# Seven half-sized products in the place of eight for every other pair of feature blocks

## The chip, the core and the metric

The kernel runs on one core of a Trainium2 chip, in one launch. The metric is the device time in microseconds. PE is TensorE (matmuls), DVE VectorE, ACT ScalarE, POOL GpSimd, SP the engine that issues the DMAs.

## What is computed

One sequence of 512 tokens with 1024 features goes through a first block (two kinds of attention, then an MLP) and through two layers of a second block, each a swiglu, a mixer of three branches and a second swiglu. All is float32. The parts that the change touches are the MLP (once) and the swiglu (four times):

```python
# first block
h2 = rmsnorm(x, ln2_g[l])
x = x + jnp.square(jax.nn.relu(h2 @ w_up[l])) @ w_down[l]      # 1024 -> 4096 -> 1024
...
def _swiglu(u, wi, wo):
    a, g = jnp.split(u @ wi, 2, axis=-1)                        # 1024 -> 2 x 1408
    return (jax.nn.silu(a) * g) @ wo                            # 1408 -> 1024
...
for l in range(DEPTH_2):
    x = x + 0.5 * _swiglu(_rms_norm(x, ffn1_norm[l]), ffn1_wi[l], ffn1_wo[l])
    ...   # the mixer
    x = x + 0.5 * _swiglu(_rms_norm(x, ffn2_norm[l]), ffn2_wi[l], ffn2_wo[l])
```

## The kernel before

x is kept in SBUF by feature: eight blocks of 128 features on the partitions, 512 tokens along them. A float32 product is made of three matmuls of type float32r: every operand is split into hi, its rounded value, and lo, the rest, and `mm3` (line 389) adds hi·hi, hi·lo and lo·hi into one PSUM bank. The split costs one ACT instruction (hi, a cast) and one DVE instruction (lo, a subtraction): for x in `split_x`, with the gain g of the norm, giving `xh` and `xl`; for weights in `load_w`, which fetches `wraw` in pieces of 128 x 1024 numbers and makes `whi` and `wlo`; for results in `split_to`. There are two raw buffers and four of whi and of wlo, taken in turn (WB).

`fm` makes one block of 128 output features for all 512 tokens: eight blocks of input features times three matmuls of 512 columns, 24 in all. The norm's factor for each token is not known when x is split; `norm_job` finds it while PE works on (a chain of small DVE instructions from the PSUM tile `ssq` to the tiles `dg`, from which the matmul `bcps` spreads it over the partitions as `Rrow`). Evacuations that need `Rrow` are held until then (`hold`), and released in one go.

`swiglu` (line 570) has eleven steps j. Each loads 128 columns of a and 128 of g, makes `pa` and `pg`, and evacuates: DVE multiplies both by `Rrow`, ACT takes silu, POOL multiplies the two, and the result is split into hidh and hidl. `mlp` (line 609) has three groups gi of 11, 11 and 10 blocks. Each group loads two blocks at a time, makes `pu` for each, and evacuates with relu and `Rrow` on DVE (`r`), a square on ACT (hidh), a square on POOL (`rq`) and a subtraction on DVE (hidl); then `down` multiplies the group's hid by w_down and adds to x.

Larger tiles live in `Slots`: 22 places of 4096 bytes a partition (kind D), given out by the first free place in a list and put back at its end. PE's instructions keep the order in which the code is written, where `Loom` weaves side jobs in at fixed points; the other engines' order is set by a list scheduler, and each engine serves its own instructions strictly in that order.

Of the kernel before, what the change touches and what calls it, by code (L numbers as in the profile page):

```python
# [19 lines left out]
KB = 8  # L20
# [3 lines left out]
FFN = 1408  # L24
# [4 lines left out]
def dram(t, off, ap):  # L29
    return bass.AP(tensor=t.tensor, offset=t.offset + off, ap=ap)  # L30
# [125 lines left out]
class Net:  # L156
    def __init__(self, ctx, tc, a):
        self.tc, self.nc, self.a = tc, tc.nc, a
        P = lambda name, bufs, **k: ctx.enter_context(tc.tile_pool(name=name, bufs=bufs, **k))
        self.const = P("const", 1)  # L160
        self.wp = P("wp", 2)
        self.act = P("act", 1)
        self.sc = P("sc", 2)
        self.tiny = P("tiny", 2)
        self.ps = P("ps", 8, space=PSUM)
        ctx.enter_context(tc.manual_schedule(engines={mybir.EngineType.PE}))
        self.loom = Loom()
# [8 lines left out]
        self.odd = False  # L176
        self.make_consts()


# [21 lines left out]
        return self.ps.tile([128, S], F32, name=name, tag="ps")  # L201


    def mm(self, out, lhsT, rhs, start, stop):
        self.nc.tensor.matmul(out, lhsT, rhs, start=start, stop=stop)  # L205
# [337 lines left out]
    def square(self, tb, t, ssq):  # L543
        A = self.nc.scalar
        junk = self.H.get("xj", [128, D])
        A.activation(junk, t, AF.Square, accum_out=ssq[:, tb:tb + 1])
        self.H.put(junk, t)

    def x_tok_job(self, out):
        for tb in range(TB):  # L550
            yield lambda: self.H.room(4096)
            t = self.H.get("xtok", [128, D])
            for h in range(2):
                ps = self.bank("xtp")
# [4 lines left out]
            yield 10.0  # L559

    def split_to(self, hi, lo, t):
        self.nc.scalar.copy(hi, t)
# [4 lines left out]
        hp = [self.pair("hid") for _ in range((n + 1) // 2)]  # L567
        return hp, self.blocks(hp, n)

    def swiglu(self, wi):  # L570
        nc = self.nc
        hp, hid = self.hid(11)
        for j in range(11):
            parts = self.load_w(wi, 2 * FFN, 0, KB, j * 128, 128, FFN + j * 128)
            pa, pg = self.bank("pa"), self.bank("pg")
            self.fm(parts, self.xs, 0, pa)
            self.fm(parts, self.xs, 1, pg)

            def evac(j=j, pa=pa, pg=pg):
                t1 = self.scr("t1")  # L580
                t2 = self.scr("t2")
                nc.vector.tensor_mul(t1, pa, self.rrow)
                nc.scalar.activation(t1, t1, AF.Silu)
                nc.vector.tensor_mul(t2, pg, self.rrow)
                nc.gpsimd.tensor_mul(t2, t2, t1)  # L585
                self.split_to(hid[j][0], hid[j][1], t2)
            self.hold(evac)
        return hp, hid
# [19 lines left out]

    def mlp(self, wu, wd, g_next):
        nc = self.nc  # L610
        j0 = 0
        for gi, n in enumerate((11, 11, 10)):
            hp, hid = self.hid(n)
            j = 0
            while j < n:
                w = min(2, n - j)
                parts = self.load_w(wu, 4096, 0, KB, (j0 + j) * 128, 128 * w)
                for i in range(w):
                    ps = self.bank("pu")
                    self.fm(parts, self.xs, i, ps)  # L620

                    def evac(ps=ps, hi=hid[j + i][0], lo=hid[j + i][1]):
                        r = self.scr("r")
                        q = self.scr("rq")
                        nc.vector.scalar_tensor_tensor(r, ps, 0.0, self.rrow, op0=ALU.max, op1=ALU.mult)
                        nc.gpsimd.tensor_mul(q, r, r)
                        nc.scalar.activation(hi, r, AF.Square)
                        nc.vector.tensor_sub(lo, q, hi.bitcast(F32))
                    self.hold(evac)
                j += w  # L630
            if gi == 2:
                self.g = g_next
            self.down(hid, wd, j0 * 128, 1.0, gi == 2)
            self.H.put(*sum(hp, ()))
            j0 += n
# [433 lines left out]
    def ffn2(self, l, which, g_next, last=False):  # L1069
        a = self.a  # L1070
        wi, wo = a[f"ffn{which}_wi_2"][l], a[f"ffn{which}_wo_2"][l]
        xtok = []
        if which == 1:
            b = a["b_in_2"][l]
            self.lcols = self.columns("lcols", [(dram(b, 0, []), 2), (dram(b, 256, []), 2), (dram(b, 768, []), 8),
                                                (dram(b, 3240, []), 24), (a["ml_conv_b_2"][l], 8), (a["ml_conv_w_2"][l], 32),
                                                (a["mla_q_norm_2"][l], 2), (a["mla_kv_norm_2"][l], 1)], 30.0)
        if last:
            self.loom.add(self.x_tok_job(xtok))
        hp, hid = self.swiglu(wi)  # L1080
# [580 lines left out]
    def everything(self):  # L1661
# [43 lines left out]
WB = (2, 4)  # L1705
```

## Time and profile before

| | us |
|---|---|
| median of 3 runs | 2325.81 (2325.63 to 2326.12) |
| the profiled execution | 2324.79 |
| its span, from the first to the last instruction | 2323.1 |
| PE busy | 2308.8 (99%), 10884 matmuls |
| DVE busy | 1293.6 (56%) |
| ACT busy | 907.3 (39%) |
| POOL busy | 381.3 (16%) |

A row of the timeline gives the start in us from the span's start, the duration, the engine, the line, the operation, the tiles as out<-in, and in brackets how long the engine sat idle before it and what it waited for. Matmuls overlap, so that their durations add up to more than the time they take. The MLP runs from 378.4 us to 723.9, the first swiglu starts there, the one behind the mixer of layer 0 at 1341.3.

### The profile page before, as it was taken

The numbers are of one execution on the slowest core, as the hardware profiler recorded it, in microseconds if no ns is written. First come the engines' busy times: TensorE is split into PE (matmuls) and PEld (weight loads), VectorE is DVE, ScalarE is ACT, GpSimd is POOL, SyncE is SP. The second block draws the span as 40 slices with busy tenths as digits, with TensorE's granted clock in tenths as the row PEclk, the third lists the DMA queues.
The fourth block names the chain that finished last, engine by engine and source line by source line (L and its number), as shares of the span: only waits on it lengthen the run. The fifth ranks groups of instructions, "written<-read, shape, count | busy, mean of one in ns | idle before, by whom it ended". The sixth has DMA issues, their size and how long they took to land.

```text
span 2323.1 us, 28438 instructions
## 1 busy us (share of the span) xinstructions
PE 2308.8 (99%) x10884; PEld 1913.4 (82%) x10884; DVE 1293.6 (56%) x2255; ACT 907.3 (39%) x1509; POOL 381.3 (16%) x385
## 2 busy tenths in 40 slices
PE   8999999999999999999999999999999999999999
PEld 7898888888888888877888888888888778888887
DVE  7844556444355545678564555455457674646552
ACT  6655432222223233656533333223236672333331
POOL 2000024101022112111111311211211101213110
PEclk9999999999999999999999999999999999999999
DMA  4223333233323323313323333333233142323332
GB/s 139 65 64 87 105 100 93 91 99 101 98 86 105 99 89 95 102 55 91 105 64 91 109 91 91 100 92 100 91 102 91 46 114 73 88 83 105 93 100 87
DMA packets 250524, 213.68 MB, mean 92 GB/s; under 512 B 14230, under 2 KB 234132, under 8 KB 250388
## 3 DMA queue, kind: packets, MB, share of 16 engines
q1 hardware_dynamic: 250388, 211.87, 30.6%
q8 instruction: 85, 1.39, 0.2%
q14 instruction: 51, 0.42, 0.1%
HBM read 208.64 MB, written 3.19 MB: 91 GB/s over the span
## 4 chain that ended last, share of the span: by engine, by line
PE 98%; DVE 1%; DMA 0%; ACT 0%; issue 0%; SPq 0%; ACTq 0%
PE pgate L205 15%; PE pd L205 15%; PE pt L205 14%; PE pg L205 10%; PE pa L205 10%; PE pu L205 8%; PE pf L205 6%; PE po L205 6%; PE pbr L205 5%; PE mls L205 1%; PE mnum L205 1%; PE sbl L205 1%; PE mss L205 1%; PE dio L205 1%; PE s L205 1%; PE pT L212 0%
## 5 line engine op out<-in xcount | busy, mean ns | idle before, releaser
L385 DVE TENSOR_TENSOR wlo<-wraw,whi 128x1024 fp32r<-128x1024 f32 (+3 forms) x394 | 550.8, 1398 | 414.1 <-ACT whi L384 409.8
L384 ACT CAST whi<-wraw 128x1024 fp32r<-128x1024 f32 (+3 forms) x394 | 404.3, 1026 | 657.2 <-PE pg L205 141.7
L205 PE MATMUL pd<-hidh,wlo 128*128 128x512 f32 x520 | 202.4, 389 | 0.0
L205 PE MATMUL pd<-hidl,whi 128*128 128x512 f32 x520 | 202.4, 389 | 0.0
L205 PE MATMUL pd<-hidh,whi 128*128 128x512 f32 x520 | 202.4, 389 | 0.0
L205 PE MATMUL pgate<-xh,whi 128*128 128x512 f32 x512 | 201.5, 394 | 0.0
L205 PE MATMUL pgate<-xh,wlo 128*128 128x512 f32 x512 | 199.6, 390 | 0.0
L205 PE MATMUL pgate<-xl,whi 128*128 128x512 f32 x512 | 199.4, 389 | 0.0
L205 PE MATMUL pt<-whi,xh 128*128 128x512 f32 (+2 forms) x480 | 182.2, 380 | 0.1
L205 PE MATMUL pt<-whi,xl 128*128 128x512 f32 (+2 forms) x480 | 172.5, 359 | 0.0
L205 PE MATMUL pt<-wlo,xh 128*128 128x512 f32 (+2 forms) x480 | 172.3, 359 | 0.0
L205 PE MATMUL pa<-xl,whi 128*128 128x512 f32 x352 | 137.3, 390 | 0.7 <-DVE xl L474 0.7
L205 PE MATMUL pa<-xh,whi 128*128 128x512 f32 x352 | 137.7, 391 | 0.0
L205 PE MATMUL pg<-xh,whi 128*128 128x512 f32 x352 | 137.5, 391 | 0.0
L205 PE MATMUL pa<-xh,wlo 128*128 128x512 f32 x352 | 137.2, 390 | 0.0
L205 PE MATMUL pg<-xh,wlo 128*128 128x512 f32 x352 | 137.1, 390 | 0.0
L205 PE MATMUL pg<-xl,whi 128*128 128x512 f32 x352 | 137.1, 389 | 0.0
L585 POOL TENSOR_TENSOR t<-t,t 128x512 f32<-128x512 f32 x44 | 56.8, 1290 | 426.5 <-ACT whi L384 303.8
L205 PEld LDWEIGHTS pd<-hidl,whi 128*128 128x128 f32 x520 | 97.6, 188 | 20.4
L205 PEld LDWEIGHTS pd<-hidh,whi 128*128 128x128 f32 x520 | 97.6, 188 | 20.2
L205 PEld LDWEIGHTS pd<-hidh,wlo 128*128 128x128 f32 x520 | 97.6, 188 | 20.1
L205 PEld LDWEIGHTS pt<-whi,xh 128*128 128x128 f32 x480 | 102.7, 214 | 13.0 <-issue 3.0
(519 smaller groups left out, 4612.8 us busy)
## 6 DMA issues: line engine op xcount, KB each, us to landing
wraw<-in_w_in_dram SPq DMA_DIRECT2D x116, 512.0 KB
wraw<-in_ffn_wi_dram SPq DMA_DIRECT2D x176, 256.0 KB
wraw<-in_ffn_wo_dram SPq DMA_DIRECT2D x34, 512.0 KB
wraw<-in_w_up_dram SPq DMA_DIRECT2D x32, 512.0 KB
wraw<-in_w_out_dram SPq DMA_DIRECT2D x24, 512.0 KB
wraw<-in_w_down_dram SPq DMA_DIRECT2D x24, 512.0 KB
wraw<-in_w_in_dram SPq DMA_DIRECT2D x32, 256.0 KB
wraw<-in_ffn_wo_dram SPq DMA_DIRECT2D x12, 384.0 KB
```

What stands on the lines that cost most here:

```text
L205: self.nc.tensor.matmul(out, lhsT, rhs, start=start, stop=stop)
L384: nc.scalar.copy(hi, raw)
L385: nc.vector.tensor_sub(lo, raw, hi.bitcast(F32))
L585: nc.gpsimd.tensor_mul(t2, t2, t1)
```

## The change

Two blocks of output features and the two halves of the tokens form a 2 x 2 product: x by halves of features and tokens (A11, A12, A22 and so on, 512 features by 256 tokens), the weights by halves of features and the two blocks (E11, E21, E22, ...). `seven` makes the four results by seven products of quarters instead of eight. It needs sums of quarters of x (S2, N1, S3, S4), which `forms` makes and splits once for each MLP and swiglu, and sums of quarters of the weights (T1 to T4 in the tiles tA and tB), which `load_sums` makes on DVE for each pair before they are split. Each product is 4 x 3 matmuls of 256 columns into half a bank. The order of the products on PE is A11·E11 (bank a), S2·T2 (b), A22·T4 (d), N1·T1 (c), A12·E21 (added onto a, once ACT has copied it as s1, a half of the tile m7), S3·T3 (added onto b, once DVE has made u2, the other half of m7), and later S4·E22 (added onto c, once DVE has read it). The seventh is put off into the next block (`later`, `flush`). A swiglu pair is the a and the g block of one step, for j = 2, 4, 6, 8; an MLP pair is two neighbouring blocks, for seven of the sixteen pairs. The sums of x hold eight places of kind D until the last pair; tA and tB hold two more from the loading of a pair to its splits.

```diff
@@ -386,11 +387,11 @@
-    def mm3(self, ps, whi, wlo, xhi, xlo, first, last):
-
-        self.mm(ps, whi, xhi, first, False)
-        self.mm(ps, whi, xlo, False, False)
-        self.mm(ps, wlo, xhi, False, last)
+    def mm3(self, ps, whi, wlo, xhi, xlo, first, last, **k):
+
+        self.mm(ps, whi, xhi, first, False, **k)
+        self.mm(ps, whi, xlo, False, False, **k)
+        self.mm(ps, wlo, xhi, False, last, **k)
...
+    def forms(self):
...
+        names = ("S2", "N1", "S3", "S4")
+        self.sums = {n: tuple(H.get("sum" + n, [128, 4, 256], F32R) for _ in range(2)) for n in names}
+        half = slice(0, 256), slice(256, 512)
+        for i in range(2):
+            f = {n: self.scr("f" + n).rearrange("p (k c) -> p k c", c=256) for n in names}
+            t = self.scr("ft").rearrange("p (k c) -> p k c", c=256)
+            for j in range(2):
+                k1, k2 = 2 * i + j, 4 + 2 * i + j
+                x = lambda k, h: self.x[:, k, half[h]]
+                A.activation(t[:, j], x(k1, 1), AF.Copy, scale=g[:, k1:k1 + 1])
+                for n, k, h, sc, other in (("N1", k2, 1, g, t), ("S2", k1, 0, ng, f["N1"]), ("S3", k1, 0, g, t),
+                                           ("S4", k2, 0, ng, f["S2"])):
+                    V.scalar_tensor_tensor(f[n][:, j], x(k, h), sc[:, k:k + 1], other[:, j], op0=ALU.mult, op1=ALU.subtract)
+            for n in names:
+                hi, lo = (y[:, 2 * i:2 * i + 2] for y in self.sums[n])
+                self.split_to(hi, lo, f[n])
...
+    def load_sums(self, w, ncol, c0, c1):
...
+        (r1, v1), (r2, v2) = E
+        ta, tb = (H.get(n, [128, 2, 4, 128]) for n in ("tA", "tB"))
+        V.tensor_add(ta[:, 1], v1[:, :, 1], v2[:, :, 1])
+        V.tensor_add(tb[:, 0], ta[:, 1], v1[:, :, 0])
+        V.tensor_add(tb[:, 1], tb[:, 0], v2[:, :, 0])
+        V.tensor_add(ta[:, 0], v1[:, :, 0], v1[:, :, 1])
...
+        A.copy(h11, v1[:, :, 0])
+        V.tensor_sub(l11, v1[:, :, 0], h11.bitcast(F32))
...
+        split(flat(tb), 1024, ("T2", "T4"), lambda i, k: i * 512 + k * 128)
+        split(flat(ta), 1024, ("T1", "T3"), lambda i, k: i * 512 + k * 128)
+        split(r2, 1024, ("E21", "E22"), lambda i, k: k * 256 + i * 128)
+        H.put(ta, tb)
+        return out
+
+    def seven(self, w, ncol, c0, c1, u, v, done):
...
+        W = self.load_sums(w, ncol, c0, c1)
+        a, b, c, d = (self.bank("ps7")[:, 0:256] for _ in range(4))
+        m = self.scr("m7")
+        s1, u2 = m[:, 0:256], m[:, 256:512]
+        u3 = self.scr("u7")[:, 0:256]
+
+        def prod(ps, q, e, first):
+            for k in range(4):
+                self.mm3(ps, *W[e][k], *self.quarters[q][k], first and k == 0, k == 3, skip_group_check=not first)
+            self.loom.turn()
+        prod(a, "A11", "E11", True)
+        A.copy(s1, a)
+        self.flush()
+        prod(b, "S2", "T2", True)
+        V.tensor_add(u2, b, s1)
+        prod(d, "A22", "T4", True)
+        prod(c, "N1", "T1", True)
+        prod(a, "A12", "E21", False)
+        prod(b, "S3", "T3", False)
+        V.tensor_add(u3, b, s1)
+        V.scalar_tensor_tensor(v[:, 256:512], c, -1.0, u3, op0=ALU.mult, op1=ALU.subtract)
+        V.tensor_add(u[:, 256:512], d, u3)
+
+        def rest():
+            prod(c, "S4", "E22", False)
+            V.scalar_tensor_tensor(v[:, 0:256], c, -1.0, u2, op0=ALU.mult, op1=ALU.subtract)
+            done(a)
+        self.later.append(rest)
...
+    def swiglu(self, wi, last):
...
         for j in range(11):
+            if j == 1:
+                self.forms()
+            if j in SEVEN:
+                self.loom.wait(lambda: self.normed)
...
+                self.seven(wi, 2 * FFN, j * 128, FFN + j * 128, t1, t2, done)
...
             self.fm(parts, self.xs, 0, pa)
+            self.flush()
...
             while j < n:
                 w = min(2, n - j)
+                if gi == 0 and j == 2:
+                    self.forms()
+                if w == 2 and (gi, j) in SEVEN_MLP:
+                    self.loom.wait(lambda: self.normed)
...
+                    self.seven(wu, 4096, c, c + 128, u, v, done)
...
                     self.fm(parts, self.xs, i, ps)
+                    self.flush()
...
+            self.flush()
             if gi == 2:
+                self.drop_forms()
...
+SEVEN = (2, 4, 6, 8)
+SEVEN_MLP = {(0, 4), (0, 8), (1, 0), (1, 4), (1, 8), (2, 2), (2, 6)}
```

In the last swiglu the job that transposes x back to tokens moves from the beginning to the steps behind the last pair.

Three places in the order of the instructions follow. The first is DVE in the MLP's first group, from the evacuations that were held for `Rrow`. Before (pu is a block's result, rq POOL's square):

```order
L467 COPY Rrow_3682<-bcps_3679 128x512
L625 SCALAR_TENSOR_TENSOR r_3684<-pu_3576,Rrow_3682 128x512
L625 SCALAR_TENSOR_TENSOR r_3690<-pu_3601,Rrow_3682 128x512
L628 TENSOR_TENSOR hidl_3553<-rq_3685,hidh_3552 128x512
L625 SCALAR_TENSOR_TENSOR r_3708<-pu_3666,Rrow_3682 128x512
L628 TENSOR_TENSOR hidl_3553<-rq_3691,hidh_3552 128x512
```

With the change, DVE from the split of the first pair's E21 and E22 (wlo_3826) to u2 (m7_3833, made of bank b, ps7_3830, and s1):

```order
L564 TENSOR_TENSOR wlo_3826<-wraw_3805,whi_3825 128x1024
L759 TENSOR_TENSOR hidl_3553<-rq_3742,hidh_3552 128x512
L787 SCALAR_TENSOR_TENSOR r_3746<-pu_3601,Rrow_3738 128x512
L386 TENSOR_TENSOR wlo_3914<-wraw_3912,whi_3913 128x1024
L759 TENSOR_TENSOR hidl_3553<-rq_3748,hidh_3552 128x512
L787 SCALAR_TENSOR_TENSOR r_3764<-pu_3722,Rrow_3738 128x512
L583 TENSOR_SCALAR ng_11597<-gains_327 128x8
L787 SCALAR_TENSOR_TENSOR r_3795<-pu_3770,Rrow_3738 128x512
L386 TENSOR_TENSOR wlo_3920<-wraw_3918,whi_3919 128x1024
L759 TENSOR_TENSOR hidl_3555<-rq_3766,hidh_3554 128x512
L759 TENSOR_TENSOR hidl_3555<-rq_3797,hidh_3554 128x512
L666 TENSOR_TENSOR m7_3833<-ps7_3830,m7_3833 128x256
```

All four held evacuations and the next two weight splits stand between the pair's last weights and u2.

The second place is ACT at the same point. Before, casts of weights and squarings of the held blocks:

```order
L384 CAST whi_3746<-wraw_3745 128x1024
L384 CAST whi_3752<-wraw_3751 128x1024
L627 ACTIVATE hidh_3552<-r_3684 128x512
L627 ACTIVATE hidh_3552<-r_3690 128x512
L627 ACTIVATE hidh_3554<-r_3708 128x512
L384 CAST whi_3820<-wraw_3819 128x1024
```

With the change, ACT from the cast of E21 and E22 to s1 (m7_3833, the copy of bank a, ps7_3829):

```order
L563 CAST whi_3825<-wraw_3805 128x1024
L385 CAST whi_3913<-wraw_3912 128x1024
L758 ACTIVATE hidh_3552<-r_3740 128x512
L758 ACTIVATE hidh_3552<-r_3746 128x512
L385 CAST whi_3919<-wraw_3918 128x1024
L758 ACTIVATE hidh_3554<-r_3764 128x512
L758 ACTIVATE hidh_3554<-r_3795 128x512
L663 COPY m7_3833<-ps7_3829 128x256
```

The copy s1 stands behind the four squarings and behind the casts of the next two pieces of weights.

The third place is DVE where the MLP's second group follows on down of the first; pd_4286 and pd_4321 (pd_4464 and pd_4499 with the change) are down's last two results. Before:

```order
L385 TENSOR_TENSOR wlo_4370<-wraw_4368,whi_4369 128x1024
L480 TENSOR_TENSOR x_77<-pd_4286,x_77 128x512
L385 TENSOR_TENSOR wlo_4376<-wraw_4374,whi_4375 128x1024
L385 TENSOR_TENSOR wlo_4444<-wraw_4442,whi_4443 128x1024
L480 TENSOR_TENSOR x_77<-pd_4321,x_77 128x512
L385 TENSOR_TENSOR wlo_4450<-wraw_4448,whi_4449 128x1024
```

With the change:

```order
L640 TENSOR_TENSOR wlo_4559<-wraw_4548,whi_4558 128x512
L481 TENSOR_TENSOR x_77<-pd_4464,x_77 128x512
L481 TENSOR_TENSOR x_77<-pd_4499,x_77 128x512
L623 TENSOR_TENSOR tA_4552<-wraw_4548,wraw_4550 128x512
L626 TENSOR_TENSOR tA_4552<-wraw_4548 128x512
L624 TENSOR_TENSOR tB_4553<-tA_4552,wraw_4548 128x512
L625 TENSOR_TENSOR tB_4553<-tB_4553,wraw_4550 128x512
L564 TENSOR_TENSOR wlo_4563<-tB_4553,whi_4562 128x1024
```

The four additions and the split of T2 and T4 moved behind the update of x from down's last result, where three splits of weights stood ahead of it.

## Rows read from the trace of the kernel before

**Rows 1.** The page: busy us, share and instructions; granted clock by slices.
```profile
PE 2308.8 (99%) x10884; PEld 1913.4 (82%) x10884; DVE 1293.6 (56%) x2255; ACT 907.3 (39%) x1509; POOL 381.3 (16%) x385
...
PEclk9999999999999999999999999999999999999999
```

**Rows 2.** Waits of PE: us in total, times, longest us.
```profile
PE colT L212 <- DMA rows<-in_ln_g_dram: 4.4, 1, 4.4
...
PE pa L205 <- DVE xl L474: 0.7, 1, 0.7
```

**Rows 3.** Chain in order of time, whole span: start, us, what.
```profile
439.89 59.84 PE pd L205 x264
```

**Rows 4.** Timeline of PE at the kernel's start, matmuls of 256 columns.
```profile
10.73 1.97 PE L212 MATMUL xtp<-ident,xin 128*128 128x128 f32 x8 [4.17 <-DMA xin<-in_x_dram]
...
13.14 0.42 PE L205 MATMUL pt<-whi,xh 128*128 128x256 f32 x1
13.35 0.33 PE L205 MATMUL pt<-wlo,xh 128*128 128x256 f32 x1
...
20.52 0.28 PE L205 MATMUL pt<-wlo,xh 128*128 128x256 f32 x1
...
26.03 0.28 PE L205 MATMUL pt<-whi,xl 128*128 128x256 f32 x1
```

**Rows 5.** Groups of DVE by form: count, busy us, mean ns, idle before.
```profile
L385 DVE TENSOR_TENSOR wlo<-wraw,whi 128x1024 fp32r<-128x1024 f32 x356 | 514.1, 1444 | 363.6 <-ACT whi L384 359.3 <-PE mqp L205 3.4 <-issue 0.2
...
L1578 DVE SCALAR_TENSOR_TENSOR mlqk<-cvt,lcols,mlqk 128x510 f32<-128x510 f32 x16 | 12.0, 749 | 0.4
...
L1653 DVE SCALAR_TENSOR_TENSOR mnum<-mnum,rmly,mgo 128x128 f32<-128x128 f32 x32 | 8.8, 348 | 0.1
```

**Rows 6.** Timeline of DVE at the start of the MLP.
```profile
379.52 1.99 DVE L385 TENSOR_TENSOR wlo<-wraw,whi 128x1024 fp32r<-128x1024 f32 x1 [0.21 <-ACT whi L384]
...
387.57 0.16 DVE L438 TENSOR_SCALAR rca<-ssq 128x4 f32<-128x4 f32 x1 [4.37 <-PE ssq L205]
...
388.32 1.22 DVE L385 TENSOR_TENSOR wlo<-wraw,whi 128x1024 fp32r<-128x1024 f32 x1
389.47 0.15 DVE L444 SCALAR_TENSOR_TENSOR rcy<-rct,rcy 128x4 f32<-128x4 f32 x1
...
391.72 0.69 DVE L457 TENSOR_TENSOR dg<-ident,rcl 128x512 fp32r<-128x512 f32 x1
392.32 1.22 DVE L385 TENSOR_TENSOR wlo<-wraw,whi 128x1024 fp32r<-128x1024 f32 x1
```

**Rows 7.** Chain in order of time, the MLP behind its norm.
```profile
393.62 46.27 PE pu L205 x204
```

**Rows 8.** The start of ffn1 in layer 0: chain, and DVE's last dg.
```profile
726.75 3.24 DMA wraw<-in_ffn_wi_dram
...
743.77 0.47 PE bcps L205 x2
...
752.43 5.44 PE pa L205 x24
...
742.37 0.68 DVE L457 TENSOR_TENSOR dg<-ident,rcl 128x512 fp32r<-128x512 f32 x1
```

**Rows 9.** The start of ffn2 in layer 0: DVE's timeline, and the chain.
```profile
1350.31 0.16 DVE L438 TENSOR_SCALAR rca<-ssq 128x4 f32<-128x4 f32 x1 [4.37 <-PE ssq L205]
...
1364.54 5.44 PE pa L205 x24
```

**Rows 10.** Groups of ACT by form, columns as in rows 5.
```profile
L384 ACT CAST whi<-wraw 128x1024 fp32r<-128x1024 f32 x356 | 373.7, 1050 | 588.6 <-PE pg L205 138.2 <-PE pd L205 68.9 <-PE pt L205 67.5
...
L627 ACT ACTIVATE hidh<-r 128x512 fp32r<-128x512 f32 x32 | 20.1, 628 | 66.2 <-DVE r L625 66.0
```

**Rows 11.** The page's group of POOL; DVE's timeline behind the start of down.
```profile
L585 POOL TENSOR_TENSOR t<-t,t 128x512 f32<-128x512 f32 x44 | 56.8, 1290 | 426.5 <-ACT whi L384 303.8
...
442.81 0.68 DVE L628 TENSOR_TENSOR hidl<-rq,hidh 128x512 fp32r<-128x512 f32 x1
```

More of the change, by code (lines that the diff above doesn't have):

```diff
@@ L176, in __init__ @@
         self.odd = False
+        self.later = []
         self.make_consts()
@@ L201, in bank, with mm @@
         return self.ps.tile([128, S], F32, name=name, tag="ps")
-    def mm(self, out, lhsT, rhs, start, stop):
-        self.nc.tensor.matmul(out, lhsT, rhs, start=start, stop=stop)
+    def mm(self, out, lhsT, rhs, start, stop, **k):
+        self.nc.tensor.matmul(out, lhsT, rhs, start=start, stop=stop, **k)
         n = 1
@@ L568, in hid @@
         return hp, self.blocks(hp, n)
-    def swiglu(self, wi):
-        nc = self.nc
+    def forms(self):
+        nc, g, H = self.nc, self.g, self.H
+        V, A = nc.vector, nc.scalar
+        ng = self.tiny.tile([128, KB], F32, name="ng", tag="ng")
+        V.tensor_scalar(ng, g, -1.0, None, op0=ALU.mult)
+        names = ("S2", "N1", "S3", "S4")
[14 more added lines that the diff above has]
+                self.split_to(hi, lo, f[n])
+        q = lambda k, h: [(self.xh[:, kk, half[h]], self.xl[:, kk, half[h]]) for kk in range(4 * k, 4 * k + 4)]
+        self.quarters = {"A11": q(0, 0), "A12": q(1, 0), "A22": q(1, 1)}
+        for n in names:
+            self.quarters[n] = [(self.sums[n][0][:, k], self.sums[n][1][:, k]) for k in range(4)]
@@ new lines, in drop_forms, with split @@
+    def drop_forms(self):
+        self.H.put(*sum(self.sums.values(), ()))
+    def load_sums(self, w, ncol, c0, c1):
+        nc, H = self.nc, self.H
+        V, A = nc.vector, nc.scalar
+        E = []
+        for k0 in (0, 4):
+            raw = self.wp.tile([128, 1024], F32, name="wraw", tag="wraw", bufs=WB[0])
+            rv = raw.rearrange("p (k h c) -> p k h c", h=2, c=128)
+            for h, c in ((0, c0), (1, c1)) if c1 != c0 + 128 else ((None, c0),):
+                n = 128 if h is not None else 256
+                nc.sync.dma_start(rv[:, :, h] if h is not None else raw.rearrange("p (k c) -> p k c", c=256),
+                                  dram(w, k0 * 128 * ncol + c, [[ncol, 128], [128 * ncol, 4], [1, n]]))
+            E.append((raw, rv))
+        (r1, v1), (r2, v2) = E
[4 more added lines that the diff above has]
+        V.tensor_add(ta[:, 0], v1[:, :, 0], v1[:, :, 1])
+        out = {}
+        def split(src, n, names, pick):
+            hi = self.wp.tile([128, n], F32R, name="whi", tag="whi", bufs=WB[1])
+            lo = self.wp.tile([128, n], F32R, name="wlo", tag="wlo", bufs=WB[1])
+            self.split_to(hi, lo, src)
+            for i, name in enumerate(names):
+                out[name] = [tuple(y[:, o:o + 128] for y in (hi, lo)) for o in (pick(i, k) for k in range(4))]
+        flat = lambda t: t.rearrange("p a k c -> p (a k c)")
+        e11 = self.wp.tile([128, 512], F32R, name="whi", tag="whi", bufs=WB[1])
+        f11 = self.wp.tile([128, 512], F32R, name="wlo", tag="wlo", bufs=WB[1])
+        h11, l11 = (y.rearrange("p (k c) -> p k c", c=128) for y in (e11, f11))
+        A.copy(h11, v1[:, :, 0])
+        V.tensor_sub(l11, v1[:, :, 0], h11.bitcast(F32))
+        out["E11"] = [(e11[:, k * 128:k * 128 + 128], f11[:, k * 128:k * 128 + 128]) for k in range(4)]
+        split(flat(tb), 1024, ("T2", "T4"), lambda i, k: i * 512 + k * 128)
[3 more added lines that the diff above has]
+        return out
@@ L576, in swiglu @@
             self.fm(parts, self.xs, 0, pa)
+            self.flush()
+            if last and j > SEVEN[-1]:
+                last()
+                last = None
             self.fm(parts, self.xs, 1, pg)
@@ L581, in evac @@
                 t2 = self.scr("t2")
[L582 to L585, printed above, removed]
+                V.tensor_mul(t1, pa, self.rrow)
+                A.activation(t1, t1, AF.Silu)
+                V.tensor_mul(t2, pg, self.rrow)
+                G.tensor_mul(t2, t2, t1)
                 self.split_to(hid[j][0], hid[j][1], t2)
@@ L620, in mlp, with evac @@
                     self.fm(parts, self.xs, i, ps)
-                    def evac(ps=ps, hi=hid[j + i][0], lo=hid[j + i][1]):
+                    self.flush()
+                    def evac(ps=ps, hl=hid[j + i]):
                         r = self.scr("r")
[L624 to L628, printed above, removed]
+                        V.scalar_tensor_tensor(r, ps, 0.0, self.rrow, op0=ALU.max, op1=ALU.mult)
+                        square(r, *hl)
                     self.hold(evac)
                 j += w
+            self.flush()
             if gi == 2:
+                self.drop_forms()
                 self.g = g_next
@@ L1077, in ffn2 @@
                                                 (a["mla_q_norm_2"][l], 2), (a["mla_kv_norm_2"][l], 1)], 30.0)
-        if last:
-            self.loom.add(self.x_tok_job(xtok))
-        hp, hid = self.swiglu(wi)
+        hp, hid = self.swiglu(wi, last and (lambda: self.loom.add(self.x_tok_job(xtok))))
         if last:
```

36 lines of the change are left out of this document (35 added, 1 removed).

## The prediction

> **What bounds the kernel now.** I read the page first. PE is busy 99% of the span [rows 1]; the list of waits has PE waiting for other engines four times, from 4.4 us at the start down to 0.7 us [rows 2]; and the chain of work that ended last, in order of time, is one run of PE's matmuls behind another [rows 3, 7]. So a saved matmul is worth its time, but only while no wait takes its place; DVE, busy 56%, is the engine to watch. The granted clock is 1.00 in every slice, PE's upper level of 2.4 GHz [rows 1]. The durations that the page gives for matmuls (389 ns) overlap, so I take spacings: 264 matmuls of 512 columns took 59.84 us in the chain, 0.2267 us each [rows 3], and in the timeline 46 steps of 256 columns last from 20.52 to 26.03 us, 0.1198 us each [rows 4].
>
> **What is removed.** A pair of blocks is 48 matmuls of 512 columns before, 48 x 0.2267 = 10.88 us, and 84 of 256 after, 84 x 0.1198 = 10.06 us. That is 0.82 us a pair and, for 23 pairs (7 in the MLP, 4 in each of four swiglus), **18.8 us**. It is under the eighth that the count of products promises, because a 256-column matmul costs 53% of a 512-column one. Weight loads rise from 48 to 84 a pair and stay inside the measured spacing.
>
> The Trainium skill, "TensorE: Matmul & The Clock Gate", section "Back-to-back issue gap", has N/2.4 + 2.5 ns for one matmul after another, 109 and 216 ns here. By it a pair would save 1.2 us and all pairs 27 us. The rows differ from the page, at 120 and 227, and decide.
>
> **What is added, once the pairs run.** I price DVE by what one instruction delays the next: 0.61 us for 512 columns (391.72, then 392.32), 1.15 for 1024 (388.32, then 389.47), 0.08 less than their durations [rows 5, 6]. A swiglu pair with its ordinary neighbour wants four additions (2.4), five splits of weights of 1024 columns and one of 512 (6.4), seven pieces of 256 (2.7), and five of 512 (3.1): 14.6 us of DVE under 20.9 us of PE. In the MLP it is some 15.7, and POOL's squarings slow DVE besides. In both the queue just keeps up, and the weights of the next pair are ready 2 to 4 us early. I cost this at nothing; PE's two blocks are the cover, and where it is short by one wide split a pair loses about 1 us. The DMAs move the same bytes as before.
>
> **What is added ahead of the first pair.** forms() runs five times: 16 multiply-subtracts of 256 columns and 8 splits of 512 on DVE. No row has a three-operand instruction of 256; 128 columns take 348 ns and 510 take 749 [rows 5], so about 0.48, and 0.46 as spacing with the waits on one another. So forms() is 16 x 0.46 + 8 x 0.61 = 12.3 us. It stands in DVE's queue behind the norm chain and ahead of the held evacuations, all in the 22 us of the first two blocks or pairs, where DVE was far from full before.
>
> *MLP.* DVE's norm chain starts at 387.57 and lasts 4.8 us with a wide split inside [rows 6]; now a narrow one is there: 4.3. From there to u2, which product six waits for (it adds onto bank b), the queue holds: norm 4.3, split of T2/T4 1.15, forms 12.3, Rrow 0.61, split of T1/T3 1.15, r 0.61, then the twelve rows shown with the change, 8.2 to u2 inclusive: 28.3 us, so 415.9. POOL's squarings of r overlap the wide splits there; beside POOL such a split took 1.99 instead of 1.22 [rows 6], and two to three of them make it 417.8. ACT agrees: the copy s1, which product five waits for, stands behind four squarings and behind a cast (whi_3919) whose weights can only be fetched once the split of E21/E22 has freed its raw buffer; a fetch took 3.24 us [rows 8], casts 1.05 and squarings 0.63 [rows 10], which gives some 415. Undelayed, the first product starts at 393.62 + 36 x 0.2267 = 401.8 [rows 7] and the sixth ends 8.6 later at 410.4. Now it ends at 417.8 + 1.4 = 419.2: **9 us** lost, 6.9 if POOL disturbs nothing.
>
> *ffn2, two times.* Chain from 1350.31 [rows 9]: 4.3 + 1.15 + 12.3 + 0.61 + 1.15 for T1/T3, then four evacuation products 2.4 and the split of E21/E22 1.15, at 1373.4, or 0.8 later beside POOL. Product five needs that split at its third matmul; it and the sixth take 2.6 more: 1376.0 to 1376.9. Undelayed it is 1364.54 + 8.6 = 1373.2 [rows 9]. **3.3 us** each.
>
> *ffn1, two times.* Here the additions stand inside the norm chain: three of 0.61 and the split of T2/T4, so its end moves from 743.05 [rows 8] to 745.5, and the row broadcast bcps, due at 743.8, waits 1.5 us. Everything else then follows 745.5 as in ffn2: 765.8 to 766.6 against 752.43 + 8.6 = 761.1 [rows 8]. **5 us** in layer 0. In layer 1 a hidl stands ahead of the split and waits for POOL's product (1.29 [rows 11]) and a cast: **7 us**.
>
> Together 9 + 2 x 3.3 + 5 + 7 = 27.6 us.
>
> **What is added at the MLP's second group.** Its first pair comes straight behind down. tA and tB are taken there from places that the last hid pair of the group before held, which PE reads until down's last matmul; so DVE's four additions stand behind the last update of x. From down's end: 0.2, x 0.7, additions 2.5, cast 1.05, split 1.15, so 5.7 us, where product two wants its low half after 1.7. **4.3 us** with the latencies between (3.5 to 5). In the third group an ordinary pair lies between, 10.9 us of cover.
>
> **What is added at two starts of down.** In groups one and two the seventh product moves behind the last block's; its evacuation and that block's come together. Before, the last hidl ran 2.9 us into down [rows 11]. Now DVE has about 8.4 us of work there (two splits of weights, v twice, two hidl, r, and its wait for POOL), and PE reads block ten 7 us into down: **1.3 us** each, 0 to 1.5.
>
> **Sum.** 27.6 + 4.3 + 2.6 - 18.8 = **+15.7 us**. The profiled execution took 2324.79 (its span and 1.7 around it), 1.0 under the median of 2325.81: 2340.5 there, **2341.5** as a median.
>
> **Rivals.**
> *The cover holds (other side).* If DVE's extra work were hidden everywhere, all 18.8 us stay: 2307. For it: DVE idles 44% of the span. Against it: the idle time lies elsewhere, and a queue serves in order. It decides in the first pairs: each loses nothing only if what DVE does between the norm's start and u2 fits in 20 to 21 us, and it adds up to 23 and more.
> *The additions are cheap.* If a 256-column multiply-subtract costs hardly more than the 128-column one, 0.27 as spacing, each forms() is 3 us shorter, and with the lower ends of the other terms the losses are some 9 to 19 us: 2316 to 2327, about 2322.
> *The clock falls.* Up to six of the new waits last 2 us or more. At the kernel's start PE resumed at 10.73 after 4.17 us of waiting and ran matmuls at 0.21 apart until 13.35 and at 0.12 after [rows 4], as the lower level of 1.2 GHz would do, though the page grants 1.00 there too [rows 1]. If each wait costs that again, half of 2.6 us, it is 8 us more: 2349.
> The Trainium skill's page "TensorE: Matmul & The Clock Gate", section "HAM oscillation — how this bites in real kernels", tells of just this, a clock that falls in gaps between bursts of matmuls; no run here shows a gap in mid-kernel yet.
> *The queue does not keep up.* If the pairs behind the first lose 0.7 us each, 18 x 0.7 = 13 us: 2354.
> That the change does not do what it says: PE's count grows by 36 for each of 23 pairs, 828, as it should, so no.
>
> **How the numbers follow.** Forecast 0.52, its own range 2329 to 2350; clock 0.17; queue 0.08; cheap additions 0.13, half of it within 0.2%; cover 0.10. A measurement of this kernel can tell 0.2%, 4.65 us, from no change. Faster: 0.10 + 0.07 = 0.17. Same: 0.06 and 0.04 of the forecast's low end, 0.10. Slower: 0.73. The range of 2317 to 2356 leaves out the full cover and the far end of the queue's case.
>
> **What would show it.** Right: 256-column matmuls of ps7 0.12 us apart; PE waiting in each of the five first pairs, for ACT (m7 or whi) at product five and for DVE (m7) at product six, longest in the MLP; PE waiting about 4 us for whi and wlo behind the first group's down, and 1.5 us for dg in ffn1; pairs after the first without waits. Wrong: those waits under 2 us each (cheap additions or cover), waits spread over all pairs (queue), or a granted clock under 1.00 behind the long waits.

## The result and the profile after

The changed kernel takes 2353.86 us (median of 4 runs, 2352.77 to 2354.66) against 2325.72 (2325.52 to 2326.12): the ratio is 1.012, 95% interval 1.0103 to 1.0138. It is 28.1 us slower; 15.7 were forecast. The profiled execution took 2354.37 us, its span is 2352.7, so 29.6 more than the span of before.

The page of the changed kernel, busy time by engine and the shares of the chain that ended last:

```profile
PE 2308.2 (98%) x11712; PEld 1946.0 (83%) x11712; DVE 1451.1 (62%) x2656; ACT 976.2 (41%) x1638; POOL 415.0 (18%) x385
...
PE 86%; DVE 7%; DMA 2%; issue 2%; POOL 2%; ACT 2%; SPq 0%; DVEq 0%; POOLq 0%; ACTq 0%
```

PE issues 828 matmuls more and is busy 0.6 us less than in [rows 1], where 18.8 us were to be saved. DVE works 157.5 us more. The chain was PE's to 98% before (the line below, from the page of before); now a seventh of it is other engines and their transfers.

```profile
PE 98%; DVE 1%; DMA 0%; ACT 0%; issue 0%; SPq 0%; ACTq 0%
```

The list of waits of the changed kernel, the rows of PE (who waits for what; us in all, how often, the longest):

```profile
PE ps L206 <- ACT m L663: 17.4, 9, 7.3
...
PE ps L206 <- ACT whi L563: 3.0, 1, 3.0
PE pa L206 <- DVE wlo L386: 2.9, 2, 1.5
PE ps L206 <- DVE wlo L564: 2.3, 3, 1.7
PE bcps L206 <- DVE dg L458: 1.5, 2, 0.7
...
PE pd L206 <- DVE hidl L759: 0.7, 2, 0.5
PE ps L206 <- DVE m L666: 0.7, 1, 0.7
```

None of these seven rows has a like in [rows 2], and none waits for the sums of x themselves (sumS, sumN). ps are the banks of the seven products; m is m7, whose half s1 ACT copies before product five. Below, ffn1 is the swiglu ahead of the mixer of a layer and ffn2 the one behind it.

The second place where the time went is no wait. The page's row of the granted clock, in slices of 59 us, still reads nine tenths or more everywhere; cut out by windows, four short stretches stand at half (columns: stretch, length, busy time of PE, weight loads, DVE, ACT and POOL, granted clock, DMA share, GB/s):

```profile
410.36:420.60 10.24, 5.07 (x22) 4.77 (x23) 8.53 (x13) 3.19 (x5) 4.91 (x3) 0.50 0.44 136
512.76:519.59 6.83, 5.34 (x23) 5.05 (x24) 5.05 (x5) 3.91 (x4) 0.00 (x0) 0.50 0.44 108
1389.99:1393.40 3.41, 3.41 (x18) 3.41 (x18) 1.98 (x3) 1.31 (x3) 1.85 (x2) 0.50 0.52 154
1577.72:1584.55 6.83, 5.93 (x25) 5.74 (x26) 3.71 (x7) 2.08 (x3) 0.00 (x0) 0.50 0.52 154
```

0.50 is the lower level of 1.2 GHz. Each stretch begins in or right behind one of PE's waits, three in a first pair and one in the pair that opens the MLP's second group, and PE works 19.75 us in them at about half speed. In the first one, from PE's timeline:

```profile
407.82 0.28 PE L206 MATMUL ps<-sumN,wlo 128*128 128x256 f32 x1
415.39 0.58 PE L206 MATMUL ps<-xh,whi 128*128 128x256 f32 x1 [7.28 <-ACT m L663]
415.76 0.42 PE L206 MATMUL ps<-xl,whi 128*128 128x256 f32 x1
...
420.34 0.41 PE L206 MATMUL ps<-sumS,wlo 128*128 128x256 f32 x1
420.56 0.43 PE L206 MATMUL ps<-sumS,whi 128*128 128x256 f32 x2
420.82 0.28 PE L206 MATMUL ps<-sumS,wlo 128*128 128x256 f32 x1
```

Behind the wait a 256-column matmul takes 0.21 to 0.22 us, until 420.6, and 0.12 again from there.

**The account**, from the MLP's first matmul on. PE issues the same matmuls in the same order in the run *bare* below, which has none of these waits, so the starts of the two can be compared one by one. (A matmul's modelled end lies some 0.16 us behind the next one's earliest start, so a wait costs that much more than its listed length.) Against bare, waits cost 34.0 us, the slow clock 8.8 and shorter losses 2.2; the pairs' saving, which is what bare gains on the kernel before, brings 16.8 back. That makes, but for rounding, the 28.3 by which PE's last matmul is later than before, counted from the MLP's first. The rest of the 29.6 lies ahead of the MLP (0.5) and behind PE's last matmul (0.8).

By place, before the clock is added: the MLP's first pair 7.9, its second group 3.9, the starts of down 0.8, the first pairs of ffn1 and the block behind (with dg) 4.9 and 5.9, of ffn2 1.9 and 3.5, and pairs behind the first 5.1. The clock adds 2.2, 2.4, 1.5 and 2.7 in the four stretches.

### The profile page after: what moved, and what is told of

Read it like the earlier page. It is cut to its first block, busy times and chain, and to the rows that moved or that the text cites. A ratio compares the mean times of both kernels' runs of the same rounds, so it can differ in the third digit from the quotient of the medians.

```text
span 2352.7 us, 30616 instructions
## 1 busy us (share of the span) xinstructions
PE 2308.2 (98%) x11712; PEld 1946.0 (83%) x11712; DVE 1451.1 (62%) x2656; ACT 976.2 (41%) x1638; POOL 415.0 (18%) x385
## 4 chain that ended last, share of the span: by engine, by line
PE 86%; DVE 7%; DMA 2%; issue 2%; POOL 2%; ACT 2%; SPq 0%; DVEq 0%; POOLq 0%; ACTq 0%
PE pgate L206 15%; PE pd L206 14%; PE pt L206 14%; PE pf L206 6%; PE po L206 6%; PE ps L206 5%; PE pbr L206 5%; PE pa L206 5%; PE pg L206 5%; PE pu L206 2%; DVE fS L596 1%; POOL rq L757 1%; DVE wlo L564 1%; PE mls L206 1%; POOL t L723 1%
## 5 line engine op out<-in xcount | busy, mean ns | idle before, releaser
L386 DVE TENSOR_TENSOR wlo<-wraw,whi 128x1024 fp32r<-128x1024 f32 (+1 forms) x348 | 449.6, 1292 | 326.4 <-ACT whi L385 317.2
L385 ACT CAST whi<-wraw 128x1024 fp32r<-128x1024 f32 (+1 forms) x348 | 356.2, 1024 | 528.4 <-PE pd L206 103.6
L206 PEld LDWEIGHTS pgate<-xh,wlo 128*128 128x128 f32 x512 | 96.1, 188 | 20.3
L206 PEld LDWEIGHTS pgate<-xh,whi 128*128 128x128 f32 x512 | 96.1, 188 | 19.8
L206 PEld LDWEIGHTS pgate<-xl,whi 128*128 128x128 f32 x512 | 96.2, 188 | 19.5
L206 PE MATMUL ps<-sumS,whi 128*128 128x256 f32 x552 | 106.6, 291 | 4.1 <-ACT whi L563 3.0
L206 PEld LDWEIGHTS pt<-whi,xl 128*128 128x128 f32 x480 | 102.7, 214 | 8.4
L206 PEld LDWEIGHTS pt<-wlo,xh 128*128 128x128 f32 x480 | 103.3, 215 | 7.4 <-issue 0.5
L474 ACT ACTIVATE xh<-x,gains 128x512 fp32r<-128x512 f32 x56 | 40.4, 722 | 140.3 <-DVE x L481 73.2
```

The lines of the kernel that those rows point to most:

```text
L385: nc.scalar.copy(hi, raw)
L386: nc.vector.tensor_sub(lo, raw, hi.bitcast(F32))
L474: nc.scalar.activation(hi, self.x[:, k], AF.Copy, scale=g[:, k:k + 1])
```

## What the first pairs wait for, in the trace

In the MLP, the rows of DVE that surround the sums of x, then ACT's rows up to the copy that product five needs:

```profile
393.45 0.88 DVE L596 SCALAR_TENSOR_TENSOR fN<-x,gains,ft 128x256 f32<-128x256 f32 x2
...
404.61 0.68 DVE L468 COPY Rrow<-bcps 128x512 f32<-128x512 f32 x1
...
413.05 0.68 DVE L787 SCALAR_TENSOR_TENSOR r<-pu,Rrow 128x512 f32<-128x512 f32 x1
...
418.00 0.41 DVE L666 TENSOR_TENSOR m<-ps,m 128x256 f32<-128x256 f32 x1
```

```profile
412.10 1.04 ACT L385 CAST whi<-wraw 128x1024 fp32r<-128x1024 f32 x1 [1.06 <-DMA wraw<-in_w_up_dram]
413.77 1.30 ACT L758 ACTIVATE hidh<-r 128x512 fp32r<-128x512 f32 x2 [0.62 <-DVE r L787]
414.98 0.35 ACT L663 COPY m<-ps 128x256 f32<-128x256 f32 x1
```

The sums hold DVE from 393.45 to 404.61, 11.2 us; the held evacuations and splits of weights follow, ACT's squarings wait for DVE's r, the copy s1 stands behind the squarings, and it starts at 414.98 although bank a was ready eleven microseconds earlier. u2 begins at 418.00.

In ffn2 of layer 0 the last of the waiting is another thing (ACT, then PE):

```profile
1386.61 1.28 ACT L721 ACT_TABLE_LOAD   x1 [2.01 <-DVE t L720]
1387.90 1.15 ACT L721 ACTIVATE t<-t 128x512 f32<-128x512 f32 x2
1388.96 0.35 ACT L663 COPY m<-ps 128x256 f32<-128x256 f32 x1
```

```profile
1389.37 0.39 PE L206 MATMUL ps<-xh,whi 128*128 128x256 f32 x1 [1.76 <-ACT m L663]
```

The held evacuations start late behind the sums, and s1 stands behind the table for silu and two silu. In the prediction it was DVE's split of E21 and E22.

At the second group of the MLP, the rows of DVE, ACT and PE behind down, which ends at 509.2:

```profile
509.38 0.69 DVE L481 TENSOR_TENSOR x<-pd,x 128x512 f32<-128x512 f32 x1 [6.79 <-PE pd L206]
509.99 0.68 DVE L623 TENSOR_TENSOR tA<-wraw 128x512 f32<-128x512 f32 x1
...
511.91 0.69 DVE L625 TENSOR_TENSOR tB<-tB,wraw 128x512 f32<-128x512 f32 x1
```

```profile
512.68 1.04 ACT L563 CAST whi<-tB 128x1024 fp32r<-128x1024 f32 x1 [1.45 <-DVE tB L625]
```

```profile
513.78 0.80 PE L206 MATMUL ps<-sumS,whi 128*128 128x256 f32 x2 [3.01 <-ACT whi L563]
```

DVE had been idle 6.8 us before, but the additions come behind the last update of x, as forecast.

## The experiments

The theory: the first pairs wait because norm chain, sums of x, held evacuations and the pair's own weights stand in one stretch of DVE's (and through it ACT's) queue; the wait at the second group comes from the places of tA and tB; the slow clock is a consequence of PE's idle time. Against it stand, in turn: that a pair waits for its own additions wherever it is, that the order alone delays the second group, and that the matmuls are slow there for another reason. Medians of before in the same comparisons lay between 2325.4 and 2325.8.

**No sums of x.**

```diff
-        for i in range(2):
...
-                self.split_to(hi, lo, f[n])
         for n in names:
-            self.quarters[n] = [(self.sums[n][0][:, k], self.sums[n][1][:, k]) for k in range(4)]
+            self.quarters[n] = self.quarters["A22"]
```

> Left out: the sums of quarters of x (16 multiply-subtracts and 8 splits on DVE, their copies and casts on ACT, five times); the products take A22 in their place. Queue theory (the waits of the five first pairs come of this work standing in DVE's and ACT's queues ahead of them): those waits and the slow clock behind them go, 10.1 us in the MLP, 3.9 and 7.0 in the two first swiglus of a layer, 3.5 and 3.8 in the two second ones, 28 us together: about 2325.6 (2322 to 2330). Rival (the first pairs wait for their own additions and splits of weights and for the norm, whatever stands beside them): most of it stays, over 2345.

Measured: 2322.6 us (2320.4 to 2324.2). All waits of the first pairs are gone but those for dg, and the clock is 1.00 but for one stretch of 6.8 us behind the second group's wait, which stays as it was:

```profile
PE ps L206 <- ACT whi L563: 3.0, 1, 3.0
PE ps L206 <- ACT m L650: 1.8, 2, 1.2
PE bcps L206 <- DVE dg L458: 1.5, 2, 0.7
```

(The second row is one of the MLP's later pairs and the fourth pair of ffn2 in layer 0.) So 31 us of the changed kernel's time come of the sums of x, the slow clock behind their waits included: not their 5 x 11.2 us, of which a good part is hidden, but the delay that they hand on.

**Places of their own for tA and tB.**

```diff
+        self.tab = [H.get(n, [128, 2, 4, 128]) for n in ("tA", "tB")]
...
-        ta, tb = (H.get(n, [128, 2, 4, 128]) for n in ("tA", "tB"))
+        ta, tb = self.tab
...
-        H.put(ta, tb)
```

> tA and tB keep two places of their own through each MLP and swiglu, so that the additions of the second group's first pair need not wait until down has read the old hid. Place theory: the wait for whi and wlo behind the first group's down goes, and with it the slow clock, 6.3 us in all: about 2348 (2347 to 2349). Rival (these additions stand in DVE's queue behind the last update of x in any case, by the order alone): within 1 us of 2353.9.

Measured: 2348.05 us (2346.2 to 2348.6), 5.8 less. DVE now makes the additions while PE is in down (first and last row):

```profile
496.29 0.69 DVE L627 TENSOR_TENSOR tA<-wraw 128x512 f32<-128x512 f32 x1 [0.64 <-DMA wraw<-in_w_up_dram]
...
500.49 0.69 DVE L626 TENSOR_TENSOR tB<-tB,wraw 128x512 f32<-128x512 f32 x1
```

PE has no wait from 505 to 530 us, and the clock stays at 1.00 there. The place was the cause, not the order.

**Work in the place of waiting.**

```diff
+        def again(ps, q, e, n):
...
+            for _ in range(n):
+                for k in range(4):
+                    (wh, wl), (xh, xl) = W[e][k], self.quarters[q][k]
...
+        again(a, "A11", "E11", AGAIN.get(c0, (0, 0))[0] if ncol == 4096 else 0)
         prod(a, "A11", "E11", True)
...
+        again(c, "N1", "T1", AGAIN.get(c0, (0, 0))[1] if ncol == 4096 else 0)
         prod(c, "N1", "T1", True)
...
+AGAIN = {512: (0, 4), 1408: (2, 0)}
```

> In the MLP's first pair PE repeats the fourth product four times (48 matmuls more), and in the pair that opens the second group the first product twice (24 more), all inside the two waits of 7.4 and 3.2 us; the results are the same. Clock theory (the half-speed matmuls behind these two waits, which cost 2.24 and 2.36 us, come of PE having been idle): the extra work of 72 x 0.12 = 8.6 us fits into the waits, the granted clock stays at 1.00 there, and the time falls by 4.6 us, from 2353.9 to about 2349.3. Rival one (the matmuls there are slow for another reason, such as their operands being written at the same time): no change, 2353.9 within 1. Rival two (PE was not really waiting): plus 8.6 us, 2362.

Measured: 2351.5 us (2350.0 to 2352.4), 2.3 less, with 72 matmuls more. The times of the two kernels do not overlap, but the 95% intervals of their ratios to before do (1.0096 to 1.0126 here), so the gain is small beside the noise and the trace is the better witness. The windows around the two waits, first of this kernel, then of the changed one:

```profile
407.50:421.00 13.50, 10.58 (x85) 10.15 (x84) 10.45 (x15) 3.97 (x7) 6.76 (x4) 1.00 0.40 118
508.00:520.00 12.00, 11.08 (x87) 10.56 (x86) 8.15 (x10) 4.19 (x5) 0.00 (x0) 1.00 0.33 87
```

```profile
407.50:421.00 13.50, 6.07 (x31) 5.57 (x30) 10.85 (x15) 3.39 (x6) 6.46 (x4) 0.62 0.40 118
508.00:520.00 12.00, 8.52 (x44) 7.79 (x44) 8.23 (x10) 4.36 (x5) 0.00 (x0) 0.72 0.29 74
```

The clock stays at its upper level in both places, so idle time had lowered it, and the rival that these matmuls are slow in themselves falls. But only half of the 4.6 us comes back. At the second group 2.2 do, in the first pair 1.1. Elsewhere this trace loses 1.1 more than the changed kernel's: it has more short waits, while the 1.5 us of slow clock in ffn2 of layer 0 did not come. In the first pair PE now comes to product six early and waits there instead:

```profile
416.17 0.39 PE L206 MATMUL ps<-xh,whi 128*128 128x256 f32 x1 [1.53 <-ACT m L671]
...
419.25 0.50 PE L206 MATMUL ps<-sumS,whi 128*128 128x256 f32 x2 [1.39 <-DVE m L674]
```

u2 comes from DVE when it comes: PE goes on at 419.25, in the changed kernel at 418.47, and this trace already lies 0.8 us later when the MLP begins, so that it is the same moment. The slow clock had lain beside that wait, and half of what it cost there was not to be had.

**The first pair of each swiglu one step later.**

```diff
-SEVEN = (2, 4, 6, 8)
+SEVEN = (3, 5, 7, 9)
```

> The pairs of every swiglu are steps 3, 5, 7, 9 in the place of 2, 4, 6, 8; the sums of x are still made at step 1. Queue theory: one ordinary step more, 10.9 us of PE, covers the sums, and the waits of the first pairs and of the blocks behind them go, with the slow clock: some 20 of the 26 us that the four swiglus lose; left are the waits for dg (2.6) and what later pairs lose (2 to 4): about 2334 (2331 to 2338). Rival (a pair loses by its own additions wherever it stands, and takes the wait along): the waits are found at step 3 instead, 2350 to 2354.

Measured: 2344.2 us (2343.1 to 2346.2), 9.7 less where 20 were expected; a miss. The waits for dg are gone, those for s1 are under 0.5 us, but products one and two of the first pairs wait for their weights, 2.7 us together in three swiglus and 1.0 in the fourth, with 3.4 us at 0.50 behind one of them (ffn2 of layer 1). DVE in ffn2 of layer 0: the first sum, the row behind the last, the pair's first addition, and the split of T1 and T3:

```profile
1372.77 0.87 DVE L596 SCALAR_TENSOR_TENSOR fN<-x,gains,ft 128x256 f32<-128x256 f32 x2
...
1383.92 0.68 DVE L468 COPY Rrow<-bcps 128x512 f32<-128x512 f32 x1
...
1389.00 1.27 DVE L626 TENSOR_TENSOR tA<-wraw 128x512 f32<-128x512 f32 x1
...
1398.10 1.21 DVE L564 TENSOR_TENSOR wlo<-tA,whi 128x1024 fp32r<-128x1024 f32 x1
```

With a third block the held evacuations grow too, and the pair's additions start behind them, at 1389. From the norm chain at 1368 on DVE has one full queue; a step more of cover brings one more step's work into it.

**The low halves of the sums on POOL.**

```diff
-                self.split_to(hi, lo, f[n])
+                A.copy(hi, f[n].rearrange("p k c -> p (k c)") if False else f[n])
+                nc.gpsimd.tensor_sub(lo, f[n], hi.bitcast(F32))
```

> As the changed kernel, but the low halves of the sums of x (8 subtractions of 512 columns each time) run on POOL: DVE's 11.2 us of sums become 6.4, POOL gets 8 x 1.29 = 10.3. Queue theory (DVE's queue sets the waits): each first pair waits 2 to 5 us less, and the slow clock goes at two of the three places: some 15 us less, 2339 (2334 to 2344). Rival (ACT's queue, or the sums being late themselves, sets them; or POOL slows DVE down beside it): within 4 us of 2353.9, or above.

Measured: 2366.6 us (2366.1 to 2370.1), 12.7 more; the theory's number was missed, and the rival's warning held. One of DVE's groups of sums, first in the changed kernel, then here (shortest, median and longest duration in ns):

```profile
L596 DVE SCALAR_TENSOR_TENSOR fS<-x,ng,fN x20: 476/479/486, 394.2 to 2183.5; 128x256 f32<-128x256 f32 x20
```

```profile
L596 DVE SCALAR_TENSOR_TENSOR fS<-x,ng,fN x20: 471/992/1518, 395.1 to 2195.1; 128x256 f32<-128x256 f32 x20
```

DVE's additions wait while POOL subtracts (1300 ns in the median), so that the load taken from DVE comes back as slowness. The Trainium skill, page "SBUF — State Buffer", section "SBUF: two separate sides", says that a DVE instruction with two inputs in SBUF and a GpSimd one share a port that whichever starts first holds until it ends; these rows agree. That is not the whole loss. The low halves also come too late now, and product two of every first pair waits for them, which no row of the changed kernel does; the slow clock comes in seven stretches in the place of four:

```profile
PE ps L206 <- POOL sumS L600: 4.8, 5, 1.0
```

**Sums and pairs moved apart**, three ways. All have places of their own for tA and tB.

```diff
-            if j == 1:
-                self.forms()
+            for part, at in enumerate(AT_S):
+                if j == at:
+                    self.forms(part)
```

*forms_later*: sums whole at step 2 (MLP: third double step), swiglu pairs 4, 6, 8, five MLP pairs.

> The sums of x are made one step later (at step 2 of a swiglu, at the third double step of the MLP's first group), behind the held evacuations; first pairs come a step or more later still: swiglu pairs 4, 6, 8, MLP pairs (0,8), (1,2), (1,6), (2,2), (2,6), 17 in all; tA and tB keep places of their own. Queue theory (what made the first pairs wait was norm chain, sums, held evacuations and the pair's own weights all in one stretch of DVE): the stretches are apart now, each under 11 us of PE a step, so that almost the whole 17 x 0.82 = 13.9 us remains: about 2314 (2312 to 2319), the granted clock 1.00 everywhere. Rival (the sums cost PE time wherever they are): waits of 3 to 7 us for the first pair of each stage again, 2330 or more.

Measured: 2325.3 us (2323.7 to 2326.9), the same as before (ratio 0.999 to 1.0009) and between the theory and its rival; a miss. No slow clock, but 17 pairs still lose 10.3 us in waits: the MLP's first pair 1.7 for its low half of E11, each swiglu 1.6 to 2.7 in its pairs.

*halves*: sums in two halves at steps 1 and 2, swiglu pairs 3, 5, 7, 9, six MLP pairs from (0,6).

> The sums of x in two halves, at steps 1 and 2 of a swiglu (first pair at 3, pairs 3, 5, 7, 9) and at the second and third double step of the MLP (pairs (0,6), (1,0), (1,4), (1,8), (2,2), (2,6)), 22 pairs; tA and tB keep places of their own. Queue theory: 5.6 us of sums stand ahead of the held evacuations instead of 11.2; 22 x 0.82 = 18.0 us saved, less some 2 us of waits in each first pair: about 2317 (2312 to 2324). Rival (one step more is not enough, as the runs with late pairs alone showed): 2330 or more.

Measured: 2340.8 us (2340.2 to 2341.5); a miss. First pairs wait 3.2 to 6.7 us, and the clock falls behind four of the five, three as windows:

```profile
775.20:782.10 6.90, 5.92 (x28) 5.93 (x29) 5.40 (x7) 2.65 (x4) 0.00 (x0) 0.51 0.28 82
1574.00:1577.40 3.40, 3.40 (x18) 3.40 (x17) 3.40 (x6) 1.26 (x3) 0.00 (x0) 0.50 0.02 5
2188.40:2191.80 3.40, 3.40 (x18) 3.40 (x17) 3.27 (x5) 0.66 (x1) 0.00 (x0) 0.50 0.07 19
```

*halves_later*: the same, but in the swiglus at steps 2 and 3, with pairs 4, 6, 8.

> As the run with halves, but in a swiglu the halves are made at steps 2 and 3 and the pairs are 4, 6, 8 (18 pairs in all, 14.8 us). Queue theory: no wait of over 1 us in a swiglu, 2314 (2312 to 2318). Rival (a half made right ahead of the first pair delays the pair's own splits): waits of about 2 us for each of the four first pairs, 2320 or more.

Measured: 2329.3 us (2328.8 to 2330.9); the time was missed, while no wait in a swiglu is over 1 us, as expected. It has four pairs fewer than halves and is 11.5 us faster: in the swiglus only waits of 0.4 to 0.8 are left and no slow clock. The MLP, the same as in halves, loses 6.6 us in its first pair and 2.9 by the clock.

**A full ordinary step between the sums and the first pair.** *rested*: halves at steps 2 and 3, swiglu pairs 5, 7, 9; in the MLP halves in the first group, pairs (1,2), (1,6), (2,2), (2,6).

> The sums of x in two halves in steps where nothing is held any more (steps 2 and 3 of a swiglu, the third and fourth double step of the MLP's first group), the first pair a full ordinary step behind them: swiglu pairs 5, 7, 9, MLP pairs (1,2), (1,6), (2,2), (2,6), 16 in all; tA and tB keep places of their own. Queue theory: every stretch of DVE lies under PE's, no wait of over 1 us stays, and 16 x 0.82 = 13.1 us less some 3 us of short waits remain: about 2315.5 (2312 to 2319), faster than both kernels. Rival (each pair gives its saving back wherever it stands, by waits for its own additions and splits): 2323 to 2326.

Measured: 2314.54 us (2313.4 to 2314.6), ratio to before 0.9951 (0.9938 to 0.9965): faster than both kernels by 10.8 and 39 us. Behind the kernel's start the list of PE's waits has two rows, and neither is a pair's (three pairs still lose 0.2 to 0.3 us each, under the list's limit):

```profile
PE pT L213 <- ACT whi L385: 1.2, 1, 1.2
PE pa L206 <- DVE xl L475: 0.7, 1, 0.7
```

**Products alone.** *bare*: as without the sums of x, and without those of the weights.

> Left out: all sums, those of quarters of x and those of quarters of the weights; the products take plain quarters in their place (A22 for the sums of x, parts of the first raw tile for T1 to T4). PE's work, the splits, fetches and evacuations of all 23 pairs stay. If the count of matmuls is all that a pair brings PE: 2325.7 - 18.8 = 2306.9, plus at most 2 for the first group's end: 2307 to 2309. If a pair has a price of its own beside its sums (its evacuations, the later seventh product, four banks at once): 2311 or more.

Measured: 2308.8 us (2307.9 to 2309.5), 16.6 less than before, and no wait of 0.2 us in any pair. Counted from the MLP's first matmul, PE's last is 16.8 us earlier than before: 0.73 a pair where 0.82 was priced. In rested it is 11.3 for 16 pairs, 0.71 each.

## Why the prediction was right, and where not

Sign and range held (2317 to 2356), and the place of every large wait was named; the time lies in the upper end of the range. The forecast's own range (2329 to 2350) it missed by 4 us. It equals the time of the rival whose queue does not keep up (2354), but by chance: that rival had 13 us in the pairs behind the first, where 5.1 were found. What the forecast of 15.7 us lacked was the clock's 8.8 above all, with a saving 2.0 smaller and shorter losses of 2.2.

- **What bounds the kernel**: held. A saved matmul is worth its time when no wait takes its place (bare, rested).
- **The saving of 18.8 us**: 16.8 (bare), mis-sized by 2.0. The spacings were right (12 matmuls in 1.43 us), but a pair brings 0.73 there. Of what is missing 1.4 us shows as 5.47 us instead of 5.44 for each of the two blocks beside a pair; the rest I could not place. By the formula that the prediction cites from the Trainium skill, page "TensorE: Matmul & The Clock Gate", section "Back-to-back issue gap", it would have been some 27, an estimate. The section gives that formula for an isolated matmul and some 131 ns for a stream of 512 columns with its weight loads; the rows show 227 ns.
- **The sums of x at 12.3 us**: measured 11.2. The three-operand instruction of 256 columns follows the next after 0.40 us, 0.06 under my estimate; the rival of cheap additions (0.27) did not come.
- **The MLP's first pair, 9 us**: 7.9 in waits. s1 was put at some 415 and started at 414.98; u2's end at 417.8 was 418.4. The step held nearly to the tenth, in part by luck: the sums were 1.1 us shorter, this trace enters the MLP 0.5 us later, and DVE stood idle for POOL's squares twice, 0.93 us each, where two or three slowed splits were priced.
- **ffn1, 5 and 7 us**: 4.9 and 5.9. Of it 1.3 is the wait for dg, where 1.5 was forecast; in layer 0 another 1.6 was not in the pair but in the block behind it, which waited for its weights. As in ffn2, the pair's first wait was for s1 and not for DVE's split.
- **ffn2, 3.3 us each**: 1.9 and 3.5, but by another instruction, ACT's s1 behind silu and its table; in layer 1 1.6 of it is in the block behind. The step named the wrong engine as last; the size was near.
- **The second group, 4.3 us**: 3.9, with its cause shown by the run with fixed places.
- **The starts of down, 2.6 us**: 0.8. Product seven's evacuations were mostly in time.
- **Pairs behind the first, costed at nothing**: 5.1 us. This step failed. DVE's stretch does not end with the first pair; in ffn2 the second pairs, and in layer 0 the fourth, still wait 0.3 to 0.8 at products two and five. Without the sums of x the waits of the second pairs go, but one MLP pair, (1,8), still waits 2.2 us and two late pairs of ffn2 in layer 0 1.3 together; without the sums of weights (bare) these go too. It is 0.3 us a pair and not the 0.7 of the rival.
- **The clock, a rival with 0.17 at 8 us**: it came, at 8.8 us. This is the step that decided the miss: the waits were forecast at 34.5 us and measured at 34.0 (by luck, as the errors above cancel), and the clock was left out of the sum although up to six waits of 2 us and more were forecast and PE had run at half speed behind the one in [rows 4]. The digits of [rows 1] could not speak against it: a 9 is nine tenths or more, and the changed kernel's page has 9 throughout as well. The Trainium skill, page "TensorE: Matmul & The Clock Gate", section "HAM oscillation — how this bites in real kernels", tells of a clock that falls in gaps between bursts of matmuls; the four windows agree in kind.

Together: 34.0 of waits, 8.8 of clock and 2.2 of shorter losses, less 16.8, give the 28.3 but for rounding.

What stays open: why the clock fell behind some of the short waits and not others (below), and the same code loses differently from run to run (the MLP's pair (1,8) waited 1.1 us in the changed kernel and 2.7 where only the swiglus had been moved), so single terms are good to about 1.5 us.

## What to carry to other kernels

Cheap arithmetic that pays for fewer matmuls has to be costed by where it stands in the queues: five times 11 us of sums on an engine that idles 38% of the span cost 31 us in the end, and the same sums cost almost nothing once at least one full ordinary step lay between them, the held evacuations and the first product that needs them (in the MLP it was several). Giving a new operation one step more of cover is not enough when the same step also adds to the queue that it waits behind. Where a wait like those here (3 us and more) before a burst of matmuls is forecast, add the clock's price to it (2.2 to 2.7 us behind the three long ones of the changed kernel; less can come back, as the run with work in the wait showed), and give a buffer that is written early a place that nothing long-lived has just held.

## What the runs showed of the hardware

- The granted clock falls in mid-kernel too: behind the waits of 7.3, 3.0 and 4.3 us (2.7 and 1.7 close together) in each run that had them, and behind shorter ones not always: the wait of 1.8 us in ffn2 of layer 0 was followed by 3.4 us at 0.50 in the changed kernel, and the same wait by none in ffn2 of layer 1, nor in layer 0 of two other runs (with fixed places, and with work in the waits). In halves two waits of 1.4 and 1.5 us close together were followed by 3.4 us at 0.50 in ffn2 of layer 1 and by none in layer 0. At 0.50 a 256-column matmul takes 0.21 to 0.22 us instead of 0.12.
- Extra matmuls in two of the long waits kept the clock at 1.00 behind them; with 72 of them the kernel took 2.3 us less, little more than the noise.
- A DVE addition of 256 columns of 0.48 us took up to 1.52 beside POOL's subtractions of 512.
- A pair of the smaller matmuls brings 0.73 us (bare) where the spacings of long rows of them (0.1198 and 0.2267) give 0.82.
